# Weight rests on one engine, another order at the head of both blocks, a looped overflow path, and 1/sqrt as a power on GpSimd

## Chip, cores and metric

The kernel runs on one core of one Trainium2 chip. The metric is the device time of one execution in microseconds (us), the median of three runs.

A core has five engines with a queue of instructions each, taken in order: TensorE (PE in the profile, with PEld for the loads of its stationary operand), VectorE (DVE), ScalarE (ACT), GpSimd (POOL) and SyncE (SP), which here issues most of the DMAs. [...] SBUF is the core's memory of 128 partitions, PSUM holds what TensorE adds up.

## What is computed

Two transformer blocks one after the other on 256 tokens of width 1024, all in float32.

```python
def reference(x, ...):
    x = first_block(x, ...)      # rmsnorm, mLSTM + pooling mixer, w_out; rmsnorm, router, 32 experts (4 per token); rmsnorm
    return second_block(x, ...)  # rmsnorm, forgetting attention + gated delta rule, w_out; rmsnorm, conv FFN (2816); rmsnorm
def rmsnorm(x, g):
    return x * lax.rsqrt(jnp.mean(x * x, axis=-1, keepdims=True) + EPS) * g
def expert_block(xb, e):
    gate = jnp.minimum(xb @ w_gate[e] + b_gate[e], 7.0)
    up = jnp.clip(xb @ w_up[e] + b_up[e], -7.0, 7.0)
    return (gate * jax.nn.sigmoid(1.702 * gate) * (up + 1.0)) @ w_down[e] + b_down[e]
```

Besides the norms, 1/sqrt is needed for the heads of the mLSTM, and for queries, keys and outputs of the delta rule.

## The kernel before, in words

**Stages.** The program is unrolled and its order is written by hand. `mixer` is the first block's mixer (0 to about 134 us), `experts` the 32 experts (to about 1070), `mix2` the second block's mixer (to about 1470), `ffn2` its FFN (to the end).

**Weights.** All weights come from HBM through a `Ring` of SBUF slots of 1 MB: `add_cols` and its relatives queue jobs, `fill` issues as many as there are free slots (on SP), `refill` is called when a slot has been used. Four slots live through the kernel, eight more through block 1, and seven late ones are opened in the course of the mixer (`open_late`), at points that depend on when older tiles are done with.

**Dense products.** In both mixers and the FFN a float32 weight is split into two float32r parts: `hi`, a rounded copy that ACT makes (L372), and `lo`, the rest `w - hi` (L361), made by POOL or DVE. `prep()` (L353) does the `lo` of one piece of 128x512 and the `hi` of the next; `piece()` calls it once for each piece that TensorE takes, so that pieces are made some steps ahead. Each piece then costs three matmuls per output (hi, lo, and hi with the activations' rest; `mm3`, and the loop at L409). `lo_eng` says whose turn it is: `"g"` at the head and at the end of block 1's mixer, `"gvg"` (POOL, DVE, POOL) else. `hi` has six buffers, `lo` five.

**Order.** `run` walks through a product's pieces, and at each piece `tick` advances the small work that is queued by due time (`later`) or in the background (`start`): sinks of finished products, gates, heads, the inverse of the delta rule.

**Heads of the blocks.** Row sums of squares give `rsqrt` (L327) its input; it makes a first guess by an integer shift and refines it by two steps of four DVE instructions, ten or eleven DVE instructions in all on tiles of 128x2 to 128x16. It is called at the head of both blocks and of the FFN, in `heads()` (L769), in the router, in `end_block1`, twice in `qk_squares`, twice in `gdn_out`, and before the last scaling. `begin_dense(plan, ahead)` makes `ahead + 1` preps; then `feature_major` (L1301) scales the rows by `r` (L1310 to L1314), transposes them on TensorE (L1321) and splits them (L1326 to L1330), with `preps` between its pairs of feature blocks. In front of it `param_cols("pa", ...)` transposes the small parameters (L252), and `warm` (L1341) issues matmuls of ones.

**Overflow.** An expert takes 64 tokens. If any has more (`cmax`, L1172), the path under `tc.If` at L1173 runs, with one copy of `overflow_block` for each of three further blocks of 64; otherwise every engine jumps over that code. With these inputs nothing of it runs.

Of the kernel before, what the change touches and what calls it, by code (L numbers as in the profile page):

```python
# [20 lines left out]
E = 32  # L21
CAP = 64
# [4 lines left out]
class Ring:  # L27
# [40 lines left out]

    def add_cols(self, w, c0, n, kpt, k_total):

        for k0 in range(0, k_total, kpt):
            kk = min(kpt, k_total - k0)
            self.add((
                lambda t, kk=kk: t[:, :kk * n].rearrange("p (k c) -> p k c", k=kk),
                w[k0 * 128:(k0 + kk) * 128, c0:c0 + n].rearrange("(k p) c -> p k c", p=128),
            ))

# [15 lines left out]
class Kernel:  # L93
    def __init__(self, ctx, tc, a, dbg=None, stop=None):
        self.ctx, self.tc, self.nc, self.a = ctx, tc, tc.nc, a
        self.dbg = dbg or {}
        self.stop = stop
        self.now, self.tasks, self.bg = 0, [], []
        self.split_n = 0

# [71 lines left out]
    def consts(self):  # L172
        nc, a = self.nc, self.a
        c = self.c
        self.ones = c.tile([128, 128], F32, name="ones")
        nc.vector.memset(self.ones, 1.0)
        self.ident = c.tile([128, 128], F32, name="ident")
        nc.vector.memset(self.ident, 0.0)
        nc.gpsimd.affine_select(out=self.ident, in_=self.ident, pattern=[[-1, 128]], compare_op=OP.not_equal,
                                fill=1.0, base=0, channel_multiplier=1)  # L180
        self.lower_sum(self.rows)
        self.tris = c.tile([128, 128], BF16, name="tris")
        self.ones16 = c.tile([128, 128], BF16, name="ones16")
# [8 lines left out]

    def param_rows(self, name, *parts):

        t = self.rows.tile([128, 128], F32, name=name + "_rows")
        row = 0
        for key, src, n in parts:
            self.nc.sync.dma_start(out=t[row:row + n, :], in_=src)
            self.pcol.setdefault(key, (name, row))
            row += n  # L200
        self.prow[name] = (t, row)
        self.pt[name] = self.c.tile([128, row], F32, name=name)

    def load_early(self):
        a, c = self.a, self.c
        self.pcol, self.prow, self.pt = {}, {}, {}
        self.param_rows("pa", ("norm1", a["norm1_g"].rearrange("o (k p) -> (o k) p", p=128), 8),
                        ("conv", a["conv_w"].rearrange("o i (k p) -> (o i k) p", p=128), 32),
                        ("hng", a["head_norm_g"].rearrange("o (k p) -> (o k) p", p=128), 4),
                        ("psc", a["pool_scale"].rearrange("o (k p) -> (o k) p", p=128), 4))  # L210
        self.gbias = c.tile([128, 8], F32, name="gbias")
        self.nc.sync.dma_start(out=self.gbias[:, 0:4], in_=a["ig_b"].to_broadcast([128, 4]))
        self.nc.sync.dma_start(out=self.gbias[:, 4:8], in_=a["fg_b"].to_broadcast([128, 4]))

# [75 lines left out]
    def solver_consts(self, c):  # L290
        nc = self.nc
# [7 lines left out]
        self.bmask = c.tile([128, 8, 16], F32, name="bmask")  # L299
        nc.gpsimd.memset(self.bmask, 1.0)  # L300
        keep(self.bmask, [[-16, 8], [0, 16]], ((0, 1), (15, -1)))
# [5 lines left out]
        self.lmask = c.tile([128, 2, 64], F32, name="lmask")  # L307
        nc.gpsimd.memset(self.lmask, 1.0)
        for i in range(2):
# [17 lines left out]
    def rsqrt(self, ss, n, eps, mul=1.0, name="r", more=None):  # L327

        v = self.nc.vector
        w = ss.shape[1]  # L330
        m = self.small.tile([128, 32], F32, tag="nm", name="nm")[:, :w]
        r = self.small.tile([128, 32], F32, tag="n" + name, name="n" + name)[:, :w]
        q = self.small.tile([128, 32], F32, tag="nq", name="nq")[:, :w]
        if more is None:
            v.tensor_scalar(out=m, in0=ss, scalar1=1.0 / n, scalar2=eps, op0=OP.mult, op1=OP.add)
        else:
            v.scalar_tensor_tensor(out=m, in0=ss, scalar=eps, in1=more, op0=OP.add, op1=OP.add)
        v.tensor_scalar(out=q.bitcast(I32), in0=m.bitcast(I32), scalar1=1, scalar2=None, op0=OP.logical_shift_right)
        v.tensor_scalar(out=r.bitcast(I32), in0=q.bitcast(I32), scalar1=-1.0, scalar2=float(0x5f3759df), op0=OP.mult,
                        op1=OP.add)  # L340

        c = 0.375 ** 0.5
        for _ in range(2):
            v.tensor_tensor(out=q, in0=r, in1=r, op=OP.mult)
            v.scalar_tensor_tensor(out=q, in0=q, scalar=c, in1=m, op0=OP.mult, op1=OP.mult)
            v.scalar_tensor_tensor(out=q, in0=q, scalar=-1.25 / c, in1=q, op0=OP.add, op1=OP.mult)
            v.scalar_tensor_tensor(out=r, in0=q, scalar=1.875, in1=r, op0=OP.add, op1=OP.mult)
        if mul != 1.0:
            v.tensor_scalar(out=r, in0=r, scalar1=mul, scalar2=None, op0=OP.mult)
        return r  # L350


    def prep(self):  # L353

        nc = self.nc
        if self.half:
            hi, src, n, slot_done = self.half
            lo = self.wlo.tile([128, PIECE], F32R, tag="lo", name="lo")
            eng = nc.vector if self.lo_eng[self.split_n % len(self.lo_eng)] == "v" else nc.gpsimd
            self.split_n += 1  # L360
            eng.tensor_tensor(out=lo[:, :n], in0=src, in1=hi[:, :n].bitcast(F32), op=OP.subtract)  # L361
            if slot_done:
# [131 lines left out]
    def plan_stream(self):  # L494
# [5 lines left out]
        for c0, n in ((2048, 520), (0, 512), (512, 512), (1024, 512), (1536, 512)):  # L500
            r.add_cols(w_in, c0, n, 4, KD)
        for k0 in (512, 0):
# [55 lines left out]
    def mixer(self, block1):  # L558
        nc, tc, a = self.nc, self.tc, self.a
        v, g_ = nc.vector, nc.gpsimd  # L560
        with ExitStack() as ctx:
# [25 lines left out]
            r0 = self.rsqrt(s0[:, 0:2], 1, 1e-5, more=s0[:, 2:4])  # L587
            self.lo_eng = "g"
            self.begin_dense([(4, 520)] * 2 + [(4, 512)] * 12, PREP1[0])
            self.lo_eng = "gvg"  # L590
            self.param_cols("pa", psb, "b")
# [211 lines left out]
            self.until(lambda: "st" in done)  # L803
            self.lo_eng = LO1
            self.start(self.expert_biases(qk[:, 0:4, :].rearrange("p (i e) t -> p i (e t)", i=2)))
# [135 lines left out]
    def top_gates(self, ps):  # L941
# [24 lines left out]
    def expert_biases(self, stage):  # L966
# [201 lines left out]
    def overflow(self, xn, psx, psg, psy, pst):  # L1168
# [16 lines left out]

    def overflow_block(self, xn, e, blk, psx, psg, psy, pst):
        nc, a, x, q = self.nc, self.a, self.x, self.mow
# [159 lines left out]
    def mix2(self):  # L1347
# [3 lines left out]
        with ExitStack() as ctx:  # L1351
# [28 lines left out]
            r = self.rsqrt(s1, 1, 1e-11, more=s2)  # L1380
            self.lo_eng = "g"
            plan = [(4, n) for _, n in IN2 for _ in range(2)] + [(4, 512)] * 16
# [3 lines left out]
            self.begin_dense(plan, PREP2[0])  # L1386
            self.lo_eng = "gvg"
            hn = self.feature_major(p, x, r, FV.rearrange("p j h d -> p j (h d)"), psb, "b", "normmix", "hn", PREP2[1:])

# [625 lines left out]
    def build(self):  # L2015
# [106 lines left out]
```

## Time and profile before

| | us |
|---|---|
| median of 3 runs (1673.5 to 1675.21) | 1674.8 |
| the profiled execution | 1674.57 |
| its span, from the first instruction to the last | 1672.9 |
| PE busy in it | 1578.2 |
| DVE busy | 646.8 |
| ACT busy | 530.6 |
| POOL busy | 391.3 |

The profile is of one execution. Busy time is an average over stages with different limits, so the stages have to be read one by one.

### The profile page before, as it was taken

The numbers are of one execution on the slowest core, as the hardware profiler recorded it, in microseconds if no ns is written. First come the engines' busy times: TensorE is split into PE (matmuls) and PEld (weight loads), VectorE is DVE, ScalarE is ACT, GpSimd is POOL, SyncE is SP. The second block draws the span as 40 slices with busy tenths as digits, with TensorE's granted clock in tenths as the row PEclk, the third lists the DMA queues.
The fourth block names the chain that finished last, engine by engine and source line by source line (L and its number), as shares of the span: only waits on it lengthen the run. The fifth ranks groups of instructions, "written<-read, shape, count | busy, mean of one in ns | idle before, by whom it ended". The sixth has DMA issues, their size and how long they took to land. (4 is left out here: it accounts for less than half of the span.)

```text
span 1672.9 us, 22804 instructions
## 1 busy us (share of the span) xinstructions
PE 1578.2 (94%) x8810; PEld 960.3 (57%) x8811; DVE 646.8 (39%) x1285; ACT 530.6 (32%) x1151; POOL 391.3 (23%) x377
## 2 busy tenths in 40 slices
PE   8889999999999999999999998799998999999997
PEld 8765333333333333333333322489888989889996
DVE  5852121212212121212121121378764365665554
ACT  4643111111111111111111110256662356566654
POOL 4560000000000000000000010255464244556663
PEclk9999999999999999999999999999999999999999
DMA  7668999999999999999999999734342233455651
GB/s 278 259 258 305 367 418 421 421 421 422 420 421 422 421 421 421 422 421 421 421 421 421 421 422 421 308 126 152 127 149 80 100 125 128 153 187 185 194 182 71
DMA packets 119221, 508.33 MB, mean 304 GB/s; under 512 B 10347, under 2 KB 33700, under 8 KB 70084
## 3 DMA queue, kind: packets, MB, share of 16 engines
q1 hardware_dynamic: 117636, 506.04, 77.0%
q8 instruction: 71, 1.16, 0.3%
q10 hardware_dynamic: 1472, 0.79, 0.2%
q14 instruction: 42, 0.34, 0.1%
HBM read 505.74 MB, written 1.05 MB: 303 GB/s over the span
## 5 line engine op out<-in xcount | busy, mean ns | idle before, releaser
L361 POOL TENSOR_TENSOR lo<-w,hi 128x512 fp32r<-128x512 f32 (+2 forms) x262 | 350.3, 1347 | 332.7 <-ACT hi L107 154.2
L107 ACT ACTIVATE hi<-w 128x512 fp32r<-128x512 f32 (+2 forms) x380 | 235.7, 629 | 134.9 <-PE ps_d L110 115.8
L110 PE MATMUL ps_y<-w,ht 128*64 128x512 f32 x1024 | 230.1, 597 | 30.6 <-DVE ht L1095 25.1
L1095 DVE COPY ht<-ps_t 128x512 f32<-128x512 f32 x32 | 22.1, 692 | 595.3 <-PE ps_t L1093 595.3
L110 PE MATMUL ps_g<-w,xg 128*64 128x512 f32 x1024 | 239.8, 603 | 5.4 <-DMA w<-in_w_gate_dram 4.3
L110 PE MATMUL ps_u<-w,xg 128*64 128x512 f32 x1024 | 238.0, 600 | 2.3 <-DMA w<-in_w_up_dram 2.3
L1048 POOL COPY og<-og 128x64 f32<-128x64 f32 x32 | 6.5, 236 | 832.1 <-DVE og L1045 832.1
L110 PEld LDWEIGHTS ps_y<-w,ht 128*64 128x64 f32 x1024 | 69.1, 136 | 170.9 <-issue 113.0
L107 ACT ACTIVATE xg<-ps_x,n2p 128x128 f32<-128x128 f32 x128 | 47.0, 367 | 333.5 <-PE ps_x L110 333.2
L110 PEld LDWEIGHTS ps_g<-w,xg 128*64 128x64 f32 x1024 | 67.2, 137 | 134.7 <-issue 102.5
L110 PEld LDWEIGHTS ps_u<-w,xg 128*64 128x64 f32 x1024 | 66.3, 136 | 115.9 <-issue 96.1
L361 DVE TENSOR_TENSOR lo<-w,hi 128x512 fp32r<-128x512 f32 (+2 forms) x118 | 93.3, 791 | 94.0 <-POOL lo L361 63.2
L110 PEld LDWEIGHTS ps_x<-oh,xn 128*128 128x128 f32 x512 | 68.8, 190 | 78.4 <-issue 65.7
L107 ACT ACTIVATE y<-ps_y 64x512 f32<-64x512 f32 x64 | 37.9, 592 | 187.8 <-PE ps_y L110 187.2
L110 PE MATMUL ps_x<-oh,xn 128*128 128x128 f32 x512 | 86.9, 294 | 1.0 <-DVE oh L1030 1.0
L107 ACT ACTIVATE sg<-gg 128x512 f32<-128x512 f32 x32 | 20.1, 629 | 200.1 <-DVE gg L1274 200.1
L1124 DVE TENSOR_TENSOR x<-x,ps_x 128x512 f32<-128x512 f32 x64 | 44.0, 687 | 92.6 <-PE ps_x L110 92.6
L110 PE MATMUL ps_d<-hnh,hi 128*128 128x256 f32 x448 | 78.9, 299 | 0.0
L110 PE MATMUL ps_d<-hnh,lo 128*128 128x256 f32 x448 | 72.3, 284 | 1.8 <-POOL lo L361 1.8
L110 PE MATMUL ps_d<-hnl,hi 128*128 128x256 f32 x448 | 72.0, 283 | 0.0
L110 PE MATMUL ps_x<-y,sc 128*128 128x512 f32 x128 | 59.2, 605 | 11.1 <-ACT y L107 11.1
L110 PEld LDWEIGHTS ps_d<-hnh,hi 128*128 128x128 f32 x448 | 62.9, 193 | 2.3
(441 smaller groups left out, 2294.8 us busy)
## 6 DMA issues: line engine op xcount, KB each, us to landing
w<-in_w_down_dram SPq DMA_DIRECT2D x137, 1024.0 KB
w<-in_w_gate_dram SPq DMA_DIRECT2D x128, 1024.0 KB
w<-in_w_up_dram SPq DMA_DIRECT2D x128, 1024.0 KB
w<-in_w_in_dram SPq DMA_DIRECT2D x40, 1024.0 KB
w<-in_w_up_dram SPq DMA_DIRECT2D x44, 512.0 KB
w<-in_w_out_dram SPq DMA_DIRECT2D x8, 1024.0 KB
w<-in_w_in_dram SPq DMA_DIRECT2D x4, 1040.0 KB
w<-in_w_branch_gdn_dram SPq DMA_DIRECT2D x4, 1024.0 KB
```

The lines of the kernel that those rows point to most:

```text
L107: self.nc.scalar.activation(out=out, in_=in_, func=func, **kw)
L110: self.nc.tensor.matmul(out, lhsT=lhsT, rhs=rhs, start=start, stop=stop, **kw)
L361: eng.tensor_tensor(out=lo[:, :n], in0=src, in1=hi[:, :n].bitcast(F32), op=OP.subtract)
L1048: nc.gpsimd.tensor_copy(og[:, tb, :, 2, :], og[:, tb, :, 0, :])
L1095: v.tensor_copy(ht, ps)
L1124: v.tensor_tensor(out=o, in0=o, in1=ps, op=OP.add)
```

## The change

- `prep` makes every rest `lo` on DVE; the same for the rest of the experts' biases (L987). `lo_eng`, `split_n` and `LO1` go.
- `rsqrt` is one DVE instruction for the mean plus epsilon and one POOL instruction, a power with exponent -0.5 from a constant column `nhalf`; a factor `mul` goes into the first.
- At the start, `load_early` (six small DMAs) is issued from ACT's queue and ahead of the constants; the ring's first four jobs follow the input on SP without them in between, and the first job is two DMAs of half the size.
- `PREP1` goes from (2, 0, 0, 0) to (-1, 1, 1, 1) and `PREP2` from (4, 0, 0, 0) to (0, 1, 1, 1): where three and five pieces were begun before the transposes, none and one are, and one more after each pair of feature blocks.
- The three copies of `overflow_block` become a loop over one copy, with a counter column `first_slot`.
- Two masks (L300, L308) are set on DVE.

```diff
-    def add_cols(self, w, c0, n, kpt, k_total):
+    def add_cols(self, w, c0, n, kpt, k_total, cut=1):
         for k0 in range(0, k_total, kpt):
-            kk = min(kpt, k_total - k0)
-            self.add((
-                lambda t, kk=kk: t[:, :kk * n].rearrange("p (k c) -> p k c", k=kk),
-                w[k0 * 128:(k0 + kk) * 128, c0:c0 + n].rearrange("(k p) c -> p k c", p=128),
-            ))
+            m = kpt // (cut if not k0 else 1)
+            self.add(*[(
+                lambda t, i=i, m=m: t[:, i * n:(i + m) * n].rearrange("p (k c) -> p k c", k=m),
+                w[(k0 + i) * 128:(k0 + i + m) * 128, c0:c0 + n].rearrange("(k p) c -> p k c", p=128),
+            ) for i in range(0, kpt, m)])
...
+        self.nhalf = c.tile([128, 1], F32, name="nhalf")
+        nc.gpsimd.memset(self.nhalf, -0.5)
...
-        self.nc.sync.dma_start(out=self.gbias[:, 0:4], in_=a["ig_b"].to_broadcast([128, 4]))
+        self.nc.scalar.dma_start(out=self.gbias[:, 0:4], in_=a["ig_b"].to_broadcast([128, 4]))
...
         if more is None:
-            v.tensor_scalar(out=m, in0=ss, scalar1=1.0 / n, scalar2=eps, op0=OP.mult, op1=OP.add)
+            k = mul ** -2
+            v.tensor_scalar(out=m, in0=ss, scalar1=k / n, scalar2=k * eps, op0=OP.mult, op1=OP.add)
         else:
             v.scalar_tensor_tensor(out=m, in0=ss, scalar=eps, in1=more, op0=OP.add, op1=OP.add)
-        v.tensor_scalar(out=q.bitcast(I32), in0=m.bitcast(I32), scalar1=1, scalar2=None, op0=OP.logical_shift_right)
-        v.tensor_scalar(out=r.bitcast(I32), in0=q.bitcast(I32), scalar1=-1.0, scalar2=float(0x5f3759df), op0=OP.mult,
-                        op1=OP.add)
-        c = 0.375 ** 0.5
-        for _ in range(2):
-            v.tensor_tensor(out=q, in0=r, in1=r, op=OP.mult)
-            v.scalar_tensor_tensor(out=q, in0=q, scalar=c, in1=m, op0=OP.mult, op1=OP.mult)
-            v.scalar_tensor_tensor(out=q, in0=q, scalar=-1.25 / c, in1=q, op0=OP.add, op1=OP.mult)
-            v.scalar_tensor_tensor(out=r, in0=q, scalar=1.875, in1=r, op0=OP.add, op1=OP.mult)
-        if mul != 1.0:
-            v.tensor_scalar(out=r, in0=r, scalar1=mul, scalar2=None, op0=OP.mult)
+        self.nc.gpsimd.tensor_tensor(out=r, in0=m, in1=self.nhalf.to_broadcast([128, w]), op=OP.pow)
         return r
...
-            eng = nc.vector if self.lo_eng[self.split_n % len(self.lo_eng)] == "v" else nc.gpsimd
-            self.split_n += 1
-            eng.tensor_tensor(out=lo[:, :n], in0=src, in1=hi[:, :n].bitcast(F32), op=OP.subtract)
+            nc.vector.tensor_tensor(out=lo[:, :n], in0=src, in1=hi[:, :n].bitcast(F32), op=OP.subtract)
...
-        g_.tensor_tensor(out=stage, in0=stage, in1=self.bias.bitcast(F32), op=OP.subtract)
+        nc.vector.tensor_tensor(out=stage, in0=stage, in1=self.bias.bitcast(F32), op=OP.subtract)
...
                 with tc.If(n > CAP):
-                    for blk in range(1, T // CAP):
-                        self.overflow_block(xn, e, blk, psx, psg, psy, pst)
+                    v.memset(self.first_slot, 0.0)
+                    with tc.For_i(1, T // CAP, 1):
+                        self.overflow_block(xn, e, psx, psg, psy, pst)
...
-        v.tensor_scalar(out=col[:, :, 0], in0=col[:, :, 0], scalar1=float(-CAP * blk), scalar2=None, op0=OP.add)
+        v.tensor_scalar(out=self.first_slot, in0=self.first_slot, scalar1=float(CAP), scalar2=None, op0=OP.add)
+        v.tensor_tensor(out=col[:, :, 0], in0=col[:, :, 0], in1=self.first_slot, op=OP.subtract)
...
+        self.load_early()
         self.consts()
         self.plan_stream()
-        self.ring.fill(1)
-        self.load_early()
         self.ring.fill(4)
...
-LO1 = "g"
-PREP1 = (2, 0, 0, 0)
-PREP2 = (4, 0, 0, 0)
+PREP1 = (-1, 1, 1, 1)
+PREP2 = (0, 1, 1, 1)
```

## Rows read from the trace of the kernel before

**Rows 1.** The page: busy time of the engines; the queue of TensorE's instructions.

```profile
PE 1578.2 (94%) x8810; PEld 960.3 (57%) x8811; DVE 646.8 (39%) x1285; ACT 530.6 (32%) x1151; POOL 391.3 (23%) x377
...
q8 instruction: 71, 1.16, 0.3%
```

**Rows 2.** Stretches: length, PE, PEld, DVE, ACT, POOL busy (count), clock, DMA share, GB/s.

```profile
105.00:110.00 5.00, 2.07 (x10) 1.34 (x8) 4.69 (x10) 0.03 (x1) 3.85 (x4) 1.00 0.30 126
110.00:115.00 5.00, 1.53 (x5) 1.21 (x6) 3.76 (x13) 0.14 (x1) 0.00 (x0) 0.70 0.24 64
...
200.00:1000.00 800.00, 762.26 (x3457) 283.58 (x3457) 164.57 (x250) 106.66 (x237) 10.37 (x30) 1.00 1.01 421
...
1100.00:1150.00 50.00, 50.00 (x377) 46.23 (x375) 38.68 (x84) 32.20 (x67) 27.64 (x22) 1.00 0.52 169
1150.00:1200.00 50.00, 50.00 (x336) 43.59 (x335) 41.08 (x102) 32.67 (x79) 23.88 (x22) 1.00 0.34 107
...
1480.00:1600.00 120.00, 120.00 (x887) 113.47 (x887) 70.83 (x115) 73.88 (x145) 76.51 (x58) 1.00 0.58 185
```

**Rows 3.** What TensorE waited for: us in total, times, longest.

```profile
PE ps_b L818 <- DVE hm L811: 6.3, 1, 6.3
...
PE ps_b L1603 <- DVE tu L1594: 4.8, 1, 4.8
PE ps_b L110 <- PEq L1173: 4.8, 1, 4.8
PE ps_b L1735 <- DVE gv L1723: 3.0, 2, 2.4
...
PE ps_d L110 <- POOL lo L361: 1.8, 1, 1.8
```

**Rows 4.** The line of the rests on both engines: ns least, median, most.

```profile
L361 POOL TENSOR_TENSOR lo<-w,hi x262: 1261/1298/2309, 10.0 to 1654.3; 128x512 fp32r<-128x512 f32 x122, 128x520 fp32r<-128x520 f32 x6, 128x528 fp32r<-128x528 f32 x3
...
L361 DVE TENSOR_TENSOR lo<-w,hi x118: 672/692/2892, 21.8 to 1655.8; 128x512 fp32r<-128x512 f32 x112, 128x520 fp32r<-128x520 f32 x3, 128x528 fp32r<-128x528 f32 x3
```

**Rows 5.** Timeline around the heads of block 1: start, us, instruction, idle before.

```profile
97.31 1.62 DVE L762 SCALAR_TENSOR_TENSOR r<-dn 128x8 f32<-128x8 f32 x1
...
98.87 9.98 POOL L361 TENSOR_TENSOR lo<-w,hi 128x512 fp32r<-128x512 f32 x8
...
106.47 1.19 DVE L344 TENSOR_TENSOR nq<-nr 128x8 f32<-128x8 f32 x1
...
113.41 1.41 PE L818 MATMUL ps_b<-ident,hm 128*128 128x128 f32 x4 [6.34 <-DVE hm L811]
```

**Rows 6.** Timeline of the head of block 1.

```profile
6.46 0.16 DVE L337 SCALAR_TENSOR_TENSOR nm<-s 128x2 f32<-128x2 f32 x1
...
8.44 0.16 DVE L347 SCALAR_TENSOR_TENSOR nr<-nq,nr 128x2 f32<-128x2 f32 x1
...
9.68 0.23 PE L252 MATMUL ps_p<-ident,pa_rows 48*128 48x48 f32 x1 [0.97 <-DMA pa_rows<-in_conv_w_dram]
...
10.07 1.41 DVE L1310 TENSOR_SCALAR qk<-x,nr 128x256 f32<-128x256 f32 x1
...
15.79 0.56 PE L110 MATMUL ps_s<-hh,hi 128*8 128x256 f32 x1
```

**Rows 7.** Branches over the overflow path, and the warm-up behind it.

```profile
L1173 PEldq COMPARE_BRANCH  x1: 5932/5932/5932, 1074.0 to 1074.0; - x1
L1173 ACTq COMPARE_BRANCH  x1: 45/45/45, 1074.5 to 1074.5; - x1
...
1080.38 5.01 PE L110 MATMUL ps_b<-ones 128*128 128x128 f32 x24 [4.84 <-PEq L1173]
```

**Rows 8.** The line of the rests alone, by stretch: DVE and POOL busy (count).

```profile
1100.00:1150.00 50.00, 7.57 (x11) 27.52 (x21) 1.00 0.52 169
1150.00:1200.00 50.00, 4.78 (x7) 20.96 (x16) 1.00 0.34 107
```

**Rows 9.** POOL by shape: its smallest instruction on two columns.

```profile
L923 POOL COPY mx<-mx 128x2 f32<-128x2 f32 x1 | 0.2, 185 | 11.5 <-DVE mx L922 11.5
```

More of the change, by code (lines that the diff above doesn't have):

```diff
@@ L98, in __init__ @@
         self.now, self.tasks, self.bg = 0, [], []
-        self.split_n = 0
     def dump(self, name, ap):
@@ L191, in lower_sum, with param_rows @@
                                      base=0, channel_multiplier=-1)
-    def param_rows(self, name, *parts):
+    def param_rows(self, name, *parts, eng=None):
         t = self.rows.tile([128, 128], F32, name=name + "_rows")
@@ L197, in param_rows @@
         for key, src, n in parts:
-            self.nc.sync.dma_start(out=t[row:row + n, :], in_=src)
+            (eng or self.nc.sync).dma_start(out=t[row:row + n, :], in_=src)
             self.pcol.setdefault(key, (name, row))
@@ L209, in load_early @@
                         ("hng", a["head_norm_g"].rearrange("o (k p) -> (o k) p", p=128), 4),
-                        ("psc", a["pool_scale"].rearrange("o (k p) -> (o k) p", p=128), 4))
+                        ("psc", a["pool_scale"].rearrange("o (k p) -> (o k) p", p=128), 4), eng=self.nc.scalar)
         self.gbias = c.tile([128, 8], F32, name="gbias")
-        self.nc.sync.dma_start(out=self.gbias[:, 0:4], in_=a["ig_b"].to_broadcast([128, 4]))
-        self.nc.sync.dma_start(out=self.gbias[:, 4:8], in_=a["fg_b"].to_broadcast([128, 4]))
+        self.nc.scalar.dma_start(out=self.gbias[:, 0:4], in_=a["ig_b"].to_broadcast([128, 4]))
+        self.nc.scalar.dma_start(out=self.gbias[:, 4:8], in_=a["fg_b"].to_broadcast([128, 4]))
     def load_late(self):
@@ L299, in solver_consts @@
         self.bmask = c.tile([128, 8, 16], F32, name="bmask")
-        nc.gpsimd.memset(self.bmask, 1.0)
+        nc.vector.memset(self.bmask, 1.0)
         keep(self.bmask, [[-16, 8], [0, 16]], ((0, 1), (15, -1)))
@@ L307, in solver_consts @@
         self.lmask = c.tile([128, 2, 64], F32, name="lmask")
-        nc.gpsimd.memset(self.lmask, 1.0)
+        nc.vector.memset(self.lmask, 1.0)
         for i in range(2):
@@ L332, in rsqrt @@
         r = self.small.tile([128, 32], F32, tag="n" + name, name="n" + name)[:, :w]
-        q = self.small.tile([128, 32], F32, tag="nq", name="nq")[:, :w]
         if more is None:
-            v.tensor_scalar(out=m, in0=ss, scalar1=1.0 / n, scalar2=eps, op0=OP.mult, op1=OP.add)
+            k = mul ** -2
+            v.tensor_scalar(out=m, in0=ss, scalar1=k / n, scalar2=k * eps, op0=OP.mult, op1=OP.add)
         else:
             v.scalar_tensor_tensor(out=m, in0=ss, scalar=eps, in1=more, op0=OP.add, op1=OP.add)
-        v.tensor_scalar(out=q.bitcast(I32), in0=m.bitcast(I32), scalar1=1, scalar2=None, op0=OP.logical_shift_right)
-        v.tensor_scalar(out=r.bitcast(I32), in0=q.bitcast(I32), scalar1=-1.0, scalar2=float(0x5f3759df), op0=OP.mult,
-                        op1=OP.add)
-        c = 0.375 ** 0.5
-        for _ in range(2):
-            v.tensor_tensor(out=q, in0=r, in1=r, op=OP.mult)
-            v.scalar_tensor_tensor(out=q, in0=q, scalar=c, in1=m, op0=OP.mult, op1=OP.mult)
-            v.scalar_tensor_tensor(out=q, in0=q, scalar=-1.25 / c, in1=q, op0=OP.add, op1=OP.mult)
-            v.scalar_tensor_tensor(out=r, in0=q, scalar=1.875, in1=r, op0=OP.add, op1=OP.mult)
-        if mul != 1.0:
-            v.tensor_scalar(out=r, in0=r, scalar1=mul, scalar2=None, op0=OP.mult)
+        self.nc.gpsimd.tensor_tensor(out=r, in0=m, in1=self.nhalf.to_broadcast([128, w]), op=OP.pow)
         return r
@@ L500, in plan_stream @@
         for c0, n in ((2048, 520), (0, 512), (512, 512), (1024, 512), (1536, 512)):
-            r.add_cols(w_in, c0, n, 4, KD)
+            r.add_cols(w_in, c0, n, 4, KD, 2 if c0 == 2048 else 1)
         for k0 in (512, 0):
@@ L587, in mixer @@
             r0 = self.rsqrt(s0[:, 0:2], 1, 1e-5, more=s0[:, 2:4])
-            self.lo_eng = "g"
             self.begin_dense([(4, 520)] * 2 + [(4, 512)] * 12, PREP1[0])
-            self.lo_eng = "gvg"
             self.param_cols("pa", psb, "b")
@@ L803, in mixer @@
             self.until(lambda: "st" in done)
-            self.lo_eng = LO1
             self.start(self.expert_biases(qk[:, 0:4, :].rearrange("p (i e) t -> p i (e t)", i=2)))
@@ L957, in top_gates @@
                             op0=OP.mult)
+        self.first_slot = p.tile([128, 2], F32, name="first_slot")
         self.cnt = p.tile([1, E], I32, name="cnt")
@@ L1184, in overflow, with overflow_block @@
                         pass
-    def overflow_block(self, xn, e, blk, psx, psg, psy, pst):
+    def overflow_block(self, xn, e, psx, psg, psy, pst):
         nc, a, x, q = self.nc, self.a, self.x, self.mow
@@ L1380, in mix2 @@
             r = self.rsqrt(s1, 1, 1e-11, more=s2)
-            self.lo_eng = "g"
             plan = [(4, n) for _, n in IN2 for _ in range(2)] + [(4, 512)] * 16
@@ L1386, in mix2 @@
             self.begin_dense(plan, PREP2[0])
-            self.lo_eng = "gvg"
             hn = self.feature_major(p, x, r, FV.rearrange("p j h d -> p j (h d)"), psb, "b", "normmix", "hn", PREP2[1:])
```

## The prediction

> **What bounds the kernel now.** I read the page first, then the stretches, TensorE's waits, and the timelines of the places that the diff touches. [...] From 200 to 1000 us the DMA share is 1.01 at 421 GB/s [rows 2]: the experts' weights set the pace, and no faster engine helps there. From 1100 to 1200 and from 1480 to 1600 PE is busy for all of the time with DMA at a third to a half [rows 2]: matmuls set the pace, and a change pays only where PE has a gap or is given one. [...] So I looked for PE's waits: 6.3 us for `hm` in the first block's heads, 4.8 for `tu`, 4.8 for its own sequencer after the branch at L1173, 3.0 for `gv`, 1.8 for one `lo` [rows 3]. All five are touched by this change.
>
> The timeline of the heads shows what makes the first so long. An instruction on 128x8 values in `heads()` takes 1.62 us and one of the Newton steps 1.19, while POOL makes eight `lo` without a pause from 98.87 to 108.85 [rows 5]; the same kind of instruction takes 0.16 at the kernel's head, where POOL makes none [rows 6]. 1.2 to 1.6 is the length of one `lo` on POOL, 1.3 [rows 4]: the small DVE instruction seems to wait out the POOL instruction. That is the largest thing the change takes away.
>
> **Part 1, rests on DVE.** A `lo` costs 1298 ns on POOL and 692 on DVE, and 262 are POOL's [rows 4]. DVE has 646.8 us of work in all [rows 1], so 262 x 0.69 = 181 more fit on the average; the question is the stretch. From 1100 to 1200 DVE is busy for 38.7 + 41.1 = 79.8 us [rows 2], and POOL makes 37 `lo` there [rows 8]: 37 x 0.69 = 25.5, in sum 105 of 100. That speaks against the change. What speaks for it is that DVE's own 18 `lo` are 12.4 us of the 79.8 [rows 8], so that the other 168 take 67.4, 0.40 each; those held by POOL's 48.5 us of `lo` there [rows 8] become shorter. I estimate that 12 us come back this way (a dozen small ones at about 1 us each, as in the heads) and 4 from Newton steps, so DVE needs 88 to 90 of 100: it fits, with little slack. From 1480 to 1600 it is 70.8 + at most 58 x 0.69 = 111 of 120 [rows 2]. A queue so full delays small steps by a `lo` here and there: I take +3 us for the second block, from 0 (all hidden by pieces made ahead) to +10 (half a rest late at some 30 places).
>
> **Part 2, the heads of block 1.** Without POOL's `lo` the rest of the Newton chain and the steps on 128x8 fall from about 1.3 us each to 0.16, and ten DVE instructions become two. Five or six held instructions are 6 to 7 us, which is PE's 6.34 us wait [rows 5]; behind it the low clock costs another 1 to 2 (1.41 us for four small transposes [rows 5]). Eight `lo` now stand in DVE's own queue, 5.5 us, but between the small steps. I take -7.2; bounds -5 (half of the rests fall into the chain) and -8.5 (wait and cold clock both gone).
>
> **Part 3, the head of the kernel.** Newton runs from 6.46 to 8.60 [rows 6], eleven instructions; a mean and a power replace it. The trace has no power. Its lower bound is POOL's smallest instruction, 185 ns on 128x2 [rows 9]; its upper the chain itself, 2.1 us. The count of elements is that of the copy, and a `lo` of 256 times as many columns needs only 1.3 us, so I take 0.35, near the lower end. `r` is then there 1.5 us earlier. PE waits 0.97 us for `pa_rows` until 9.68 [rows 6]; those loads now go first, from ACT's queue, and behind them the input's squares on ACT start at most some tenths later. The first scaling takes 1.41 us at 10.07 [rows 6], held by a `lo` again; with no piece begun (`PREP1[0]` = -1) it runs alone. One scaling of 128x256 then takes about 0.35 by its size against a `lo`'s 512 columns. In sum 0.5 to 1 from the loads, 1 from the scaling, 1 from the queue of three `lo`: the first dense matmul (15.79 [rows 6]) moves by -2.7, bounds -1 (the first `lo` is now made last and PE waits for it) and -4. SP's queue loses six small issues ahead of the weights, so the first weights come no later. Two masks on DVE cost nothing: they lie in the wait for the input; without that cover some tenths.
>
> Parts 2 and 3 give -9.9 in the mixer. What of it passes through the experts' stage? The stream starts earlier if slots come free earlier, and at 0.30 of its rate the DMA was waiting for slots there [rows 2]. I take 85%, -8.4; bounds 75 and 100%.
>
> **Part 4, the overflow loop.** The jump over the unused code holds PE for 5932 ns, ACT for 45 [rows 7]; that isn't the comparison, then, but the code at the target, which isn't there. PE's instructions came in 71 packets [rows 1], so one brings (8810 + 8811) / 71 = 248 of them, 16.3 KB. PE's share of one `overflow_block` is 284 instructions by the code (a float32 matmul is two passes, as 12 in `warm` are 24 [rows 7]); three make 852, over three packets, one makes 284 and some loop control. If the target lies in code already fetched, the branch costs 0.05 to 0.1 and the second block begins 5.9 - 0.1 earlier, of which 0.2 is lost again since fewer pieces were begun: -5.6. If it doesn't, the 5.9 stay, and as `PREP2` begins one piece instead of five, about +1 comes on top. A jump of 284 crosses one or two packet bounds, depending on where it starts; I give the hit 0.6.
> [...]
>
> **Part 5, the gaps of block 2.** The wait of 1.8 us for a POOL `lo` [rows 3] ends 0.6 us earlier for each rest in that queue: -1.5 (0 to -1.8). `tu`, 4.8 us [rows 3], is a chain of small DVE instructions among matmuls: contention goes, rests come into the queue, -0.5 (0 to -5). `gv` in `gdn_out`, 3.0 us in two waits [rows 3], contains two rsqrts: -3 with the cold clock behind it (-1 to -5). FFN's head and the last scaling each lose a chain of 2.1 us for 0.5: the end, where nothing hides it, -1.5, the head of the FFN, behind which PE has other work, -0.75; together -1 to -3.
>
> **Sum** against the profiled 1674.57 us (the median of the runs is 0.2 higher): -8.4 - 5.6 - 1.5 - 0.5 - 3 - 2.25 + 3 = -18.3, which gives 1656.
>
> **The rivals.**
> *The branch still misses.* Term 4 turns from -5.6 to +1: 1663. For it: 284 is more than one packet of 248. Against: the target is three times nearer. Chance 0.25.
> *Block 1's gain is lost in the weight stream.* The DMA share of 1.01 [rows 2] means that bytes decide; if the stream's start before 134 us hangs on slots that the heads don't free, -8.4 goes: 1665, and 1671 with a missed branch. Against it: the DMA idles at the heads. Chance 0.10.
> *DVE becomes the bound of block 2: slower.* Its place is the mixer of block 2, some 390 us. If POOL's contention gives nothing back, DVE needs 105 of every 100 us there, +20.6, and the gaps of part 5 in the mixer (-5) don't close: 1656 - 3 + 20.6 + 5 = 1679. It decides from an overrun of (18.3 + 3 - 5) / 390 = 4.2 us in 100. For it: the sum of busy times. Against it: 1.2 to 1.6 us for instructions of 0.16 [rows 5, 6] are time that DVE waited. Chance 0.08.
> *The power is long.* It stands on the path at about six places. At the length of a `lo` on POOL, 1.3 us, it adds 5.7: 1662. At 3.4 us each nothing is left: 1675. For it: a power is more work than a copy, and no row has one. Chance 0.07.
> [...]
>
> **How the numbers follow.** The likeliest case, all terms as taken with a hit of the branch, has 0.50: 1656, its own range 1647 to 1662 from the bounds of parts 1 to 3 and 5, which rarely lie at one end together. The other four have 0.25, 0.10, 0.08 and 0.07. About 0.2%, 3.3 us, is what a measurement of this kernel can tell from no change. Faster by more than that is all of the first two, most of the third and half of the fourth: 0.85 with something off for terms that I can't see; same 0.06; slower 0.09. The range that leaves out 2 in 10 goes from 1642 (all terms near their good bounds) to 1669 (a missed branch with half of block 1's gain).
>
> **What the profile after would show.** PE's branch at L1173 at 0.1 us or at 6; no wait on `hm` above 1 us at about 100, and DVE's 128x8 instructions at 0.2 to 0.3; the first dense matmul at 12 to 14; the power at 0.2 to 0.5 us; start of the experts' full stream 7 to 10 us earlier; DVE at 85 to 92 of 100 in block 2 with PE still full, POOL nearly idle. Wrong I would be through DVE above 95 of 100 with PE waiting on `lo`, or through a power of microseconds.

## The result, and the profile after

The changed kernel takes 1652.55 us (median of four runs, 1651.93 to 1652.88) where the kernel before takes 1674.15 (four runs, 1671.39 to 1675.21): a ratio of 0.9871, 95% interval 0.9855 to 0.9887, or 21.6 us less. The profiled execution of it took 1652.3 us, with a span of 1650.6. The forecast was 1656, faster; 1652.55 lies in its range. That the total is near is partly luck, as the parts below show: the term for the loop, -5.6, brought 0 to 2 us, and the one for block 1 was too small by 6 us.

The page after: busy time of the engines, to be read against [rows 1].

```profile
PE 1567.6 (95%) x8810; PEld 950.9 (58%) x8811; DVE 695.4 (42%) x1437; ACT 524.9 (32%) x1151; POOL 54.8 (3%) x124
```

POOL falls from 391 to 55 us, while DVE rises only from 647 to 695, although 262 rests of 0.69 us (181 us) went over to it. The rest of those 181 us, some 132, is time that DVE's instructions took longer before, and the Newton steps (24 us in the trace before). TensorE's waits after, against [rows 3]: us in total, times, longest.

```profile
PE ps_b L109 <- issue: 3.9, 1, 3.9
PE ps_d L109 <- DVE lo L349: 3.7, 4, 2.0
PE ps_b L1589 <- DVE tu L1580: 3.3, 1, 3.3
...
PE ps_s L109 <- DVE lo L349: 2.4, 2, 1.9
...
PE ps_b L803 <- DVE hm L796: 1.0, 2, 0.7
...
PE ps_b L1721 <- DVE gv L1709: 0.7, 1, 0.7
...
PE ps_b L109 <- PEq L1159: 0.4, 1, 0.4
```

The 6.3 us for `hm` are 1.0 now, the 3.0 for `gv` 0.7, the 4.8 for `tu` 3.3. The 4.8 behind the branch are 0.4, but a new wait of 3.9 us that the profile can put down to nothing ("issue") heads this part of the list, and waits for rests add up to 6.1 us where 2.1 stood (1.8 for a rest of POOL's, 0.3 for one of DVE's).

The heads of block 1, DVE and then POOL in the timeline after, against [rows 5]: start, us, instruction, idle before.

```profile
93.76 0.13 DVE L748 SCALAR_TENSOR_TENSOR r<-dn 128x8 f32<-128x8 f32 x1
...
94.25 1.25 DVE L349 TENSOR_TENSOR lo<-w,hi 128x512 fp32r<-128x512 f32 x2
...
97.76 0.17 DVE L756 TENSOR_TENSOR r<-r,nr 128x8 f32<-128x8 f32 x1 [1.77 <-POOL nr L339]
```

```profile
96.07 1.66 POOL L339 TENSOR_TENSOR nr<-nm,nhalf 128x8 f32<-128x8 f32 x1 [22.07 <-DVE nm L336]
```

The instruction that took 1.62 us takes 0.13. Two rests stand in the queue between the small steps, 1.25 us, and the power takes 1.66, in which DVE idles 1.77.

Where the time went is seen best when the start of the same matmul is looked up in both traces:

| matmul | before | after | difference |
|---|---|---|---|
| first dense one of block 1 (`ps_s<-hh,hi`) | 15.79 | 11.98 | -3.8 |
| fourth pair of features transposed | 19.14 | 15.81 | -3.3 |
| `ps_d<-hl,hi` in the middle of block 1's products | 60.59 | 52.37 | -8.2 |
| `ps_d<-hi,hh`, further on | 83.28 | 77.42 | -5.9 |
| heads, `ps_b<-ident,hm` | 113.41 | 101.94 | -11.5 |
| biases of w_down, `ps_x<-bd,gt` | 166.39 | 150.96 | -15.4 |
| warm-up at the end of the experts | 1072.25 | 1057.50 | -14.8 |
| first dense one of block 2 (`ps_s<-hnh,hi`) | 1086.72 | 1071.96 | -14.8 |
| `ps_d<-hnl,hi` ahead of the inverse | 1220.58 | 1209.99 | -10.6 |
| `ps_b<-ident,tu` | 1264.03 | 1249.93 | -14.1 |
| `ps_b<-ident,gv` | 1354.39 | 1336.65 | -17.7 |
| head of the FFN (`ps_t<-ident,tmp`) | 1475.00 | 1453.67 | -21.3 |
| end of the span | 1672.9 | 1650.6 | -22.3 |

Two rows stand out. In this pair of traces the join of the blocks, with the shortened branch, brings nothing (-14.8 on both sides). And between 1087 and 1221 block 2 loses 4.2 us.

### The profile page after: what moved, and what is told of

Same layout as the page of the kernel before. It is cut to its first block, busy times and chain, and to the rows that moved or that the text cites. A ratio compares the mean times of both kernels' runs of the same rounds, so it can differ in the third digit from the quotient of the medians.

```text
span 1650.6 us, 22396 instructions
## 1 busy us (share of the span) xinstructions
PE 1567.6 (95%) x8810; PEld 950.9 (58%) x8811; DVE 695.4 (42%) x1437; ACT 524.9 (32%) x1151; POOL 54.8 (3%) x124
## 3 DMA queue, kind: packets, MB, share of 16 engines
q8 instruction: 71, 1.16, 0.3%
## 5 line engine op out<-in xcount | busy, mean ns | idle before, releaser
L349 DVE TENSOR_TENSOR lo<-w,hi 128x512 fp32r<-128x512 f32 (+2 forms) x380 | 257.3, 691 | 56.9 <-PE ps_d L109 30.6
L106 ACT ACTIVATE hi<-w 128x512 fp32r<-128x512 f32 (+2 forms) x380 | 232.1, 628 | 74.8 <-PE ps_d L109 67.2
L109 PEld LDWEIGHTS ps_d<-hnh,lo 128*128 128x128 f32 x448 | 60.7, 188 | 4.0 <-DVE lo L349 3.8
L109 PEld LDWEIGHTS ps_d<-hnl,hi 128*128 128x128 f32 x448 | 60.8, 188 | 0.2
```

What stands on the lines that cost most here:

```text
L106: self.nc.scalar.activation(out=out, in_=in_, func=func, **kw)
L109: self.nc.tensor.matmul(out, lhsT=lhsT, rhs=rhs, start=start, stop=stop, **kw)
L349: nc.vector.tensor_tensor(out=lo[:, :n], in0=src, in1=hi[:, :n].bitcast(F32), op=OP.subtract)
```

## The experiments

Each kernel was timed in turns with the kernel before on the same chip; the ratio is to that.

**The loop undone.**

```diff
-                    with tc.For_i(1, T // CAP, 1):
+                    for _ in range(1, T // CAP):
                         self.overflow_block(xn, e, psx, psg, psy, pst)
```

> The changed kernel with three copies of the overflow block again instead of the loop. Theory: the loop brought nothing, because behind the short jump (352 ns) PE stands 3.93 us in the middle of the warm-up until one packet of instructions is there, as it stood 5.93 us at the jump before. So the branch goes back to about 5.9 us, the gap of 3.9 us vanishes, the stretch from the last warm-up matmul of the experts to the first dense matmul of block 2 stays at 14.5 us (within 1), and the time stays at 1652.6 (within 2). Rival, part 4 of the prediction: the short jump was worth 5.6 us, and the time is 1658.

Measured: 1654.6 us (1652.32 to 1655.97), ratio 0.9883 (0.9866 to 0.99). The branch on TensorE's sequencer (ns), after and with the copies:

```profile
L1159 PEldq COMPARE_BRANCH  x1: 352/352/352, 1059.2 to 1059.2; - x1
```

```profile
L1159 PEldq COMPARE_BRANCH  x1: 6072/6072/6072, 1060.6 to 1060.6; - x1
```

TensorE's timeline at the join, after and with the copies:

```profile
1057.50 3.29 PE L109 MATMUL ps_x<-ones 128*128 128x128 f32 x28
1061.24 1.24 PE L109 MATMUL ps_b<-ones 128*128 128x128 f32 x9 [0.45 <-PEq L1159]
1066.41 3.57 PE L109 MATMUL ps_b<-ones 128*128 128x128 f32 x15 [3.93 <-issue]
1069.77 2.44 PE L1309 MATMUL ps_t<-ident,fv 128*128 128x128 f32 x12
1071.96 0.36 PE L109 MATMUL ps_s<-hnh,hi 128*8 128x256 f32 x1
```

```profile
1058.85 3.29 PE L109 MATMUL ps_x<-ones 128*128 128x128 f32 x28
1067.18 5.46 PE L109 MATMUL ps_b<-ones 128*128 128x128 f32 x24 [5.05 <-PEq L1159]
1072.43 1.74 PE L1309 MATMUL ps_t<-ident,fv 128*128 128x128 f32 x12
1073.93 0.36 PE L109 MATMUL ps_s<-hnh,hi 128*8 128x256 f32 x1
```

From the start of the 28 to the first dense matmul it is 14.46 us with the loop, 15.08 with copies. The short branch, 352 ns where it takes 6072 with copies, seems to land in code that is there; nine warm-up matmuls later TensorE stands again, and the 15 behind the gap run at a granted clock of 0.50 (1066.4 to 1070.0), the lower of the two levels, 0.50 and 1.00, that the traces before and after show. What it waits for is in the DMA queues' view of 1063 to 1065 us after: packets, MB, share.

```profile
q1 hardware_dynamic: 352, 0.74, 100.8%
q8 instruction: 1, 0.02, 3.6%
...
```

One packet of q8, which I take for TensorE's instruction queue (1.16 of the 1.48 MB of both instruction queues on the page after, 78%, where PE and PEld have 17621 of 22396 instructions, 79%), and it starts inside the gap; from 1043.0 to 1063.5 none started. In all thirteen traces that have the branch, with the loop or with copies, the first such packet starts 3.3 to 4.5 us behind the start of the branch. So the theory holds in its mechanism, but its sum of exactly nothing isn't shown: the median is 2.0 us above the changed kernel's, and 1.0 above that of its second measurement further down, with intervals that overlap. Nor is the join a fixed 14.5 us. From the start of the 28 to the first dense matmul it is 12.4 to 14.5 us in six traces with the loop and 14.5 to 16.4 in three with copies; the pair in the table has the longest with the loop and the shortest with copies.

**The loop alone**, put into the kernel before (the edit of the diff above, in the other direction, with `first_slot`).

> The kernel before with one edit: the three copies of the overflow block become the loop. Theory: the jump at the end of the experts falls from 5.93 to about 0.35 us, a gap of 4 to 5 us appears behind it in the warm-up, and the time stays within 2 us of before (ratio 0.999 to 1.001). Rival, part 4 of the prediction: 5.6 us faster, ratio 0.9967 or less.

Measured: 1672.57 us (1670.26 to 1675.15) against 1673.47, ratio 0.9995 (0.9986 to 1.0004). The branch takes 353 ns, and the timeline shows the gap behind it:

```profile
1075.53 1.35 PE L110 MATMUL ps_b<-ones 128*128 128x128 f32 x10 [0.45 <-PEq L1174]
1080.20 2.80 PE L110 MATMUL ps_b<-ones 128*128 128x128 f32 x14 [3.33 <-issue]
```

The rival, -5.6, is out; by the interval a gain of up to 2.3 us is not.

**Rests on POOL again**, in the changed kernel.

```diff
-            nc.vector.tensor_tensor(out=lo[:, :n], in0=src, ...
+            eng = nc.vector if self.lo_eng[self.split_n % len(self.lo_eng)] == "v" else nc.gpsimd
+            self.split_n += 1
+            eng.tensor_tensor(out=lo[:, :n], in0=src, ...
```

(`lo_eng` is "gvg", and "g" from the end of block 1's mixer until behind the transposes of block 2. The "g" at the head of block 1 and the rest of the biases are not put back; 261 rests are on POOL, 262 before.)

> The changed kernel with the rests on the engines of before: POOL, DVE, POOL in turn, POOL alone at the heads of both blocks and the end of block 1's mixer; all else as changed. Theory: small DVE instructions wait out POOL's rests again, TensorE waits 4 to 6 us for hm in the heads, and the time is 1663 (1659 to 1668), that is, half of the gain or more hangs on the engine of the rests. Rival: the rests in DVE's own queue cost as much as POOL's contention did, and the time stays at 1652.6 within 3.

Measured: 1664.05 us (1662.34 to 1667.0), ratio 0.9945 (0.993 to 0.996); the wait for `hm` is 5.0 us. DVE in the heads:

```profile
100.74 5.99 DVE L764 TENSOR_SCALAR hm<-hm,bag,r 128x128 f32<-128x128 f32 x8
```

The same eight instructions take 2.14 us in the changed kernel. They have one large input each, so it isn't only instructions with two tensors from SBUF that POOL's rests hold. The ratio's interval is clear of the changed kernel's: 11.5 us by the medians.

**Rests on DVE alone**, in the kernel before (L361 and the biases at L987 on DVE, all else as before).

> The kernel before with one edit: every rest, and that of the biases, on DVE. Theory: 9 to 13 us faster than before, 1661 to 1665, with the wait for hm under 1.5 us, although the Newton chains stay, since without POOL's rests each of their steps takes 0.16 to 0.2 us. Rival: without the power the chains queue behind rests on DVE and the gain is under 4 us, 1670 or more.

Measured: 1657.42 us (1654.2 to 1667.13), ratio 0.9912 (0.9888 to 0.9936): more than expected, some three quarters of the whole gain. The waits for `hm` sum to 1.5 us, and the steps of the Newton chain are short, though nothing in them was changed:

```profile
97.17 0.17 DVE L344 TENSOR_TENSOR nq<-nr 128x8 f32<-128x8 f32 x1
97.37 0.17 DVE L345 SCALAR_TENSOR_TENSOR nq<-nq,nm 128x8 f32<-128x8 f32 x1
```

L344 at this place took 1.19 us before [rows 5]. From 97 to 119 us, in windows (length, then PE, PEld, DVE, ACT, POOL busy, clock, DMA share, GB/s) of the kernel before and of this one, which is some 5 to 10 us ahead by then:

```profile
97.00:119.00 22.00, 15.60 (x61) 12.28 (x60) 17.02 (x32) 9.07 (x17) 13.14 (x10) 0.84 0.60 233
```

```profile
97.00:119.00 22.00, 20.50 (x103) 16.61 (x101) 15.57 (x39) 9.52 (x22) 0.00 (x0) 1.00 0.99 400
```

Without POOL's rests TensorE goes through 103 matmuls instead of 61 in the same time, its granted clock stays at 1.00 (0.84 before), and the DMA is full (0.99) where it was at 0.60. The edit also shortens each rest, from 1.30 to 0.69 us; but before, TensorE waited for rests 2.1 us in all, so that alone can't be the 16 us.

**Newton again**, in the changed kernel (`rsqrt` as before).

> The changed kernel with the Newton steps on DVE instead of the power on POOL. The profile after has the power at 0.77 us on 128x2, 1.64 on 128x8 and 2.90 on 128x16; a Newton chain without contention is about 2 us at any of these widths. Theory: the power wins 1 us at four places of 128x2, nothing at 128x8 and loses 1 at 128x16, so the time is 1654 (1652 to 1657). Rival, the prediction's size of the power (0.35 us everywhere, 1.5 us saved at each of six places): 1660 or more. Second rival: the power is a loss, and Newton gives 1650 or less.

Measured: 1655.65 us (1654.53 to 1656.4), ratio 0.9893 (0.9876 to 0.991): 3.1 us more than with the power by the medians, within what was expected and below the prediction's 1660; the intervals of the two ratios overlap. The power after, by shape (us busy, mean ns):

```profile
L339 POOL TENSOR_TENSOR nr<-nm,nhalf 128x16 f32<-128x16 f32 x2 | 5.8, 2899 | 74.3 <-DVE st L1445 74.3
...
L339 POOL TENSOR_TENSOR nr<-nm,nhalf 128x8 f32<-128x8 f32 x3 | 4.9, 1642 | 68.1 <-DVE nm L336 68.1
L339 POOL TENSOR_TENSOR nr<-nm,nhalf 128x2 f32<-128x2 f32 x6 | 4.6, 769 | 351.7 <-DVE nm L338 351.0 <-DVE nm L336 0.7
```

**Pieces begun as before**, in the changed kernel.

```diff
-PREP1 = (-1, 1, 1, 1)
-PREP2 = (0, 1, 1, 1)
+PREP1 = (2, 0, 0, 0)
+PREP2 = (4, 0, 0, 0)
```

> The changed kernel with the pieces begun as before: PREP1 (2, 0, 0, 0) and PREP2 (4, 0, 0, 0). Theory: at the head of block 1 the rests now stand on DVE ahead of the scalings and cost 0.7 to 1.5 us there; at block 2 they hide behind the wait for instructions, and the two short waits for the first rests (0.5 and 0.4 us) vanish: in sum within 1.5 us of the changed kernel, 1652 to 1654. Rival, the prediction's share of this edit in part 3 (two of 2.7 us): 1655 or more.

Measured: 1652.38 us (1650.08 to 1654.57), ratio 0.9883 (0.9868 to 0.9897): no difference that these runs can tell. At the head of block 1 the old pieces were expected to cost 0.7 to 1.5 us; in the trace they bring 1.5. Changed, and with the old pieces:

```profile
9.85 1.59 PE L1309 MATMUL ps_t<-ident,qk 128*128 128x128 f32 x12 [0.65 <-DVE qk L1298]
11.98 0.29 PE L109 MATMUL ps_s<-hh,hi 128*8 128x256 f32 x1 [0.55 <-ACT hi L106]
...
14.63 0.29 PE L109 MATMUL ps_s<-hh,lo 128*8 128x256 f32 x1 [1.89 <-DVE lo L349]
```

```profile
11.10 1.59 PE L1309 MATMUL ps_t<-ident,qk 128*128 128x128 f32 x12 [2.31 <-DVE qk L1298]
12.45 0.36 PE L109 MATMUL ps_s<-hh,hi 128*8 128x256 f32 x1
...
13.12 0.28 PE L109 MATMUL ps_s<-hh,lo 128*8 128x256 f32 x1
```

With no piece begun the transposes start 1.25 us earlier, but TensorE then waits 1.89 us for the first rest: the stall has only changed its place, and 1.5 us are lost.

**The path left out** of the changed kernel.

```diff
-            self.overflow(xn, psx, psg, psy, pst)
```

> The changed kernel without the overflow path: the call of overflow is left out, and so is what an expert with more than 64 tokens would need (no instruction of it runs with these inputs). Theory: the whole stall behind the experts is one wait for a packet of instructions, which both forms of the jump pay; without the jump the first transposes of block 2 start as soon as the first scaled rows are there, about 6.2 us after the start of the last 28 warm-up matmuls instead of 12.3. So -5.5 to -6.5 us, 1646.5 (1645 to 1648.5). Rival: weights or rests hold the start of block 2 as well, and the gain is under 2 us.

Measured: 1647.22 us (1644.59 to 1657.04), ratio 0.9863 (0.9842 to 0.9885). By the medians it is 5.3 below the changed kernel, as expected; but one of its five runs took 1657, and the interval overlaps the changed kernel's. In the trace the gap is gone, and from the start of the 28 to the first dense matmul it is 7.0 us instead of 14.5. So the code of a path that never runs costs this kernel some 5 us with the loop, and by the two experiments above 0 to 2 more with copies.

**The jump ahead of the warm-up**, in the changed kernel, and then with a shorter warm-up behind it.

```diff
-WARM0 = 14
+WARM0 = 0
```

```diff
-WARM0 = 14
-WARM = 12
+WARM0 = 0
+WARM = 5
```

> The changed kernel with WARM0 at 0: the 28 warm-up matmuls (3.29 us) that stood ahead of the jump are gone, the 24 behind it stay. Theory: the wait for the packet counts from the jump, so all that follows comes 3.3 us earlier: 1649.3 (1648 to 1650.5), with the gap of 3.9 us behind nine warm-up matmuls as long as before. Rival: the packet comes at a time of its own (it is asked for earlier than the jump), the gap grows by 3.3 us, and the time stays at 1652.6.

> The changed kernel with WARM0 at 0 and WARM at 5: ten warm-up matmuls behind the jump instead of 24, none ahead of it. Theory: beside the 3.3 us of the earlier jump, the 15 matmuls behind the gap (3.57 us, at the lower clock level) go down to one or two, so the transposes come some 5.8 us earlier than in the changed kernel; they run at the lower level, which gives back 1 to 2 us: 1648 (1646.5 to 1649.5). Rival: the low clock lasts into the dense matmuls and gives back all that the second step brings: 1650 or more.

Measured: 1648.37 us (1646.46 to 1649.61), ratio 0.9853 (0.9839 to 0.9868), and 1650.07 (1647.5 to 1658.52), ratio 0.9881 (0.9859 to 0.9904). TensorE's timeline of the two:

```profile
1060.05 4.43 PE L109 MATMUL ps_b<-ones 128*128 128x128 f32 x24 [3.34 <-DVEq L1159]
1064.27 1.64 PE L1309 MATMUL ps_t<-ident,fv 128*128 128x128 f32 x12
1065.66 0.36 PE L109 MATMUL ps_s<-hnh,hi 128*8 128x256 f32 x1
```

```profile
1061.92 1.68 PE L109 MATMUL ps_b<-ones 128*128 128x128 f32 x10 [3.34 <-DVEq L1159]
1064.91 2.79 PE L1309 MATMUL ps_t<-ident,fv 128*128 128x128 f32 x12 [1.31 <-ACT fv L106]
1067.35 0.56 PE L109 MATMUL ps_s<-hnh,hi 128*8 128x256 f32 x1
```

The first brought 4.2 us by its medians, against 3.3 expected, but not with the gap that was expected: TensorE meets the other engines behind the branch and waits for DVE's sequencer (3.34 us), which is at its last sums until then. The packet comes in the meantime, and the gap is gone. That its arrival counts from the jump is settled by the packets: here it starts at 1059.07, after at 1063.62, with the branch at 1055.5 and 1059.2, so 3.6 and 4.4 us behind it, as in the other traces. The second kernel saved nothing more: the scaled rows weren't there (1.31 us), and the transposes and first dense matmuls ran at a granted clock of 0.50 (1064.9 to 1067.7), 0.56 us for one that takes 0.36. Its rival is right.

**Both that seemed to help**, with the changed kernel measured again beside them; and two rests on POOL beside DVE's long reduction.

> The changed kernel unaltered, as the measure for the two others of this call. 1652.5 within 2 us; its first transposes of block 2 again about 15.8 us after the start of the last eight matmuls of the experts, with the gap of about 4 us in the warm-up.

> The changed kernel with WARM0 at 0 and with the pieces begun as before, PREP1 (2, 0, 0, 0) and PREP2 (4, 0, 0, 0). Theory: both were seen to bring something at a place of their own: the jump 4 to 5 us at the start of block 2, the pieces begun early 1.5 us at the head of block 1 and 1 to 2 us of waits for the first rests of block 2. If they add, the time is 5 to 7 us below the changed kernel, 1646 (1644.5 to 1648). Rival: five rests on DVE ahead of the scalings are no longer hidden once the jump is early, and take back what the waits cost: 1648.5 or more.

```diff
+            eng = nc.gpsimd if self.pool_lo else nc.vector
+            self.pool_lo -= bool(self.pool_lo)
...
                 ad = atd.rearrange("p b h i -> p (b h) i")
+                self.pool_lo = 2
                 v.tensor_reduce(
```

> The same, and two rests on POOL while DVE makes its 3.7 us reduction in the delta rule's inverse. Theory: TensorE's longest wait for a rest in the changed kernel (2.04 us) stands behind that reduction; with two rests made on POOL beside it the wait goes: 1 to 2 us below the run without this edit. Rival: POOL's rests and DVE's work around them hold each other, as in the kernel before, and the time is the same or longer.

Measured: 1653.65 us (1651.78 to 1655.78), ratio 0.9879 (0.9864 to 0.9894) for the changed kernel; 1647.71 (1645.93 to 1648.44), ratio 0.9842 (0.9828 to 0.9855) with `WARM0` at 0 and the old pieces; 1648.68 (1645.06 to 1649.86), ratio 0.9844 (0.983 to 0.9857) with two rests on POOL as well. The second beats both kernels, 5.9 us under the changed one, with intervals that don't touch. But the jump alone had 1648.37 (0.9853): the 0.7 us that the pieces add to it can't be told from nothing. The third brings nothing: its premise had gone, since with the old pieces TensorE waits 0.4 us for rests in all, and with two on POOL 2.5.

## Why the prediction was right in the sum, and where its steps failed

**Part 4, the branch, failed.** The step "if the target lies in code already fetched, the branch costs 0.05 to 0.1 and the second block begins 5.9 - 0.1 earlier" was wrong in its conclusion. The branch did hit (0.35 us), but eight to ten matmuls behind it TensorE stood again, for 3.93 us (2.6 to 3.9 in the six traces with the loop and the warm-up of before), around the landing of one packet of instructions, and the remaining 15 warm-up matmuls then ran at a granted clock of 0.50 (3.57 us). Worth: 0 in the table above; by the medians 0.9 us for the loop alone and 1.0 to 2.0 in the changed kernel, never clear of no change, against 5.6. The packet starts 3.3 to 4.5 us behind the branch in either form, so most of what the loop saves at the branch is lost in the warm-up. That a jump of 284 instructions may find its target fetched, where one of 852 doesn't, was an estimate from the 248 that a packet brings; the branch itself bears it out, with 352 ns against 5932 before and 6072 with copies. But by the q8 packets TensorE waits for a packet behind the short branch too. The whole price, with the warm-up at a clock of 0.50, is the 5.3 us (by the medians) that the kernel without the path saves.

**Parts 2 and 3, block 1, were right in mechanism and too small.** The head gave -3.3 (-3.8 at the first dense matmul) where -2.7 was taken, though `PREP1`, from which part of it was to come, cost 1.5 us. The first scaling takes 0.34 us, as taken. The small parameters' transposes begin at 8.94 instead of 9.68, within the 0.5 to 1 taken for the loads; no run undoes the loads by themselves.

At the heads the table shows -5.9 before, -11.5 at `hm` and -15.4 behind them. The last 1.6 us of that are luck: they come at 163 us, where both kernels wait 1.1 us for `gg`, and only before was the granted clock 0.50 behind this wait (163.2 to 166.5; after it is 1.00 from 149.0 to 152.4). The heads themselves gave 8.0 where -7.2 was taken. In the trace before, nine held instructions stood on the chain, 11.0 us together, and not five or six; and the first of them, 1.62 us, met the rest of the biases and not a `lo`, and ended with it:

```profile
96.50 2.41 POOL L987 TENSOR_TENSOR qk<-qk,bias 128x1024 f32<-128x1024 f32 x1
```

What was missing is the stretch between: 2.6 us (from -3.3 to -5.9), in which the difference first grows to -8.2 and half of that growth is given back. Before, TensorE waited 2.35 us for `z` with a granted clock of 0.50 behind it (57.4 to 60.7); after, it waits 1.1 for `z` and later 1.8 for `cy`, and the 0.50 stands behind that (61.4 to 64.8).

The gain's way through the experts was put at 85%; all of it came through (-13.9 at 163 us, -14.8 at their end): the weights' stream simply starts earlier, as the full DMA at the heads shows (0.99 with the rests moved alone). With the rests moved alone the warm-up at the end of the experts starts 14.1 us earlier than before, so nearly all of block 1's gain is the rests'; single traces spread there, with Newton in the changed kernel it is 11.6. In sum -14.8 instead of -8.4, an error that hid that of part 4.

**Part 1, the queue on DVE, was right in its sign; its size is right only with what `PREP2` cost.** Stretches of block 2 after, 14 us before those of [rows 2], of all instructions and then of the rests alone (length and DVE):

```profile
1086.00:1136.00 50.00, 49.63 (x371) 45.68 (x370) 41.34 (x101) 31.21 (x65) 0.00 (x0) 1.00 0.46 150
1136.00:1186.00 50.00, 49.53 (x336) 43.27 (x335) 39.51 (x94) 31.76 (x78) 8.70 (x8) 1.00 0.39 126
```

```profile
1086.00:1136.00 50.00, 19.29 (x30) 1.00 0.46 150
1136.00:1186.00 50.00, 14.97 (x23) 1.00 0.39 126
```

DVE needs 80.9 of 100 us, not the 88 to 90 of the prediction: 34.3 for 53 rests and 46.6 for 142 others, 0.33 us each where 0.40 stood. The slower rival (DVE as the bound) did not come about. Until 1221 block 2 loses 4.2 us where +3 was taken. Of these, 1.6 are waits for rests (0.5 and 1.1), 1.4 waits for ACT and for one instruction of DVE's, and for 1.2, in which the same matmuls take longer, the profile shows no cause. With the pieces begun as before and the rests on DVE, the same stretch loses 1.9 us and has no wait for a rest; in the whole kernel there is then one:

```profile
PE ps_d L109 <- DVE lo L349: 0.4, 1, 0.4
```

Over all traces with the rests on DVE the stretch loses 3.6 to 4.8 us with the new `PREP2` (seven traces) and 1.2 to 1.9 with the old (four). So DVE's queue costs 1 to 2 us there, and the pieces begun later another 2 to 3. The longest wait for a rest comes just behind the stretch, after a reduction on DVE:

```profile
1210.49 3.72 DVE L1544 TENSOR_REDUCE atd<-tu 128x256 f32<-128x2048 f32 x1
```

```profile
1215.98 0.74 PE L109 MATMUL ps_d<-hnh,lo 128*128 128x256 f32 x4 [2.04 <-DVE lo L349]
```

It stands near the place where a rest of POOL's cost 1.8 us before, so the -1.5 of part 5 for that wait brought nothing. The old pieces spare TensorE this wait, but it then waits 2.6 us for `bsel` and 0.8 for `cf`, which come out of the same chain.

**Part 5, the gaps.** From -10.6 ahead of the inverse to -22.3 at the end it is 11.7 us where 7.25 were taken: 3.5 up to `tu`, 3.6 between it and `gv`, 3.6 more up to the head of the FFN, 0.9 behind it. Apart from POOL's rest the signs are right, the size is not. Part of what the terms miss is the clock that follows a wait. Around `gv`, before and after (windows as above):

```profile
1353.00:1362.00 9.00, 6.99 (x35) 6.75 (x36) 6.24 (x20) 3.75 (x9) 1.28 (x1) 0.62 0.00 0
```

```profile
1335.00:1344.00 9.00, 7.91 (x67) 7.53 (x66) 6.95 (x19) 4.09 (x10) 0.31 (x1) 1.00 0.32 117
```

Before, `gv` is awaited for 2.4 us and the granted clock is 0.50 from 1354.5 to 1361.2; after, it stays at 1.00, and TensorE goes through 67 matmuls instead of 35. Over the whole span the granted clock rose from 0.985 to 0.994. What belongs to the power shows in the two kernels that keep Newton with the rests on DVE. The changed kernel with Newton has the steps at `tu` and `gv` as well (3.7 and 3.0), so the power isn't needed for them. Up to the head of the FFN the step is 3.6 and 3.7 in the two traces of the changed kernel, 2.7 and 3.1 with Newton; behind it the changed kernel gains 0.9 twice, and those with Newton lose 0.3. There the power brings about 2 us, of 2.25 taken.

**The power** was mis-sized: 0.77, 1.64 and 2.90 us where 0.35 was taken. By the widths 2, 8 and 16 that is about 0.15 us a column on top of 0.5, so an element of it costs some sixty times one of a rest (1298 ns for 512 columns [rows 4]). It is worth 3.1 us in all by the medians, not 1.5 at each of six places. In [rows 6] the chain without contention took 2.1 us on 128x2; its instructions are as short on 128x8 (0.17 us), so the power wins clearly at width 2 alone. The first power of the kernel takes 0.73 us, the six on two columns 0.77 in the mean: the first call costs no more than the others.

**The contention** is what the kernel gained by: 11.5 us by the kernel that puts POOL's rests back, 16.3 by the one that moves them alone. The traces show it for instructions with two inputs, and its price: a DVE instruction of 0.13 to 0.17 us lasts until the POOL instruction that it meets is done, 1.0 to 1.6 us in the heads before. Instructions with one input are held too, some of the eight of `hm` above and one of 128x8 at 102.72 (1.21 us), but not all: the RECIPROCAL on 128x8 at 100.21 takes 0.20 us while POOL makes a rest, as it does without one. What sets it apart is not shown.

## What to carry to other kernels

Work that was moved to an idle GpSimd was not free here, where the vector engine runs chains of small instructions beside it (11.5 us by the medians, with the rests put back on POOL): look for small instructions that last as long as a large one of the neighbour, and move the large one back. A jump over code that doesn't run cost a wait for instructions here whether the branch itself was long (5.9 us) or short (0.35 us, and 3.9 us nine matmuls behind it); put it where the engine waits for another anyway, ahead of a warm-up and not behind it (4.2 us by the medians here). And check a forecast by the start of the same instruction in both traces, place by place, since a right sum can hold two wrong terms.

## What was not expected of the hardware

A branch of 352 ns with a wait of 3.93 us nine matmuls behind it, for which the trace names no cause, but in which a single instruction packet starts and ends. A power on GpSimd that costs 0.15 us a column. And the contention in the other direction, in the changed kernel: a rest on DVE takes 2.72 us instead of 0.69 while POOL multiplies two tiles of 128x1024, DVE first, then POOL.

```profile
1200.96 2.72 DVE L349 TENSOR_TENSOR lo<-w,hi 128x512 fp32r<-128x512 f32 x1
```

```profile
1200.73 5.21 POOL L1541 TENSOR_TENSOR tu<-ap,bmask 128x1024 f32<-128x1024 f32 x2 [3.01 <-DVE ap L1514]
```
